# Token sums of a hybrid attention layer: the subtractions beside values and context on VectorE, and the first pair's sums from reloaded f32 rows

## The chip, the cores and the metric

The kernel runs on one core of one Trainium2 chip. The metric is the device time of one execution in microseconds, as the median of several runs. TensorE (PE) multiplies; VectorE (DVE), ScalarE (ACT) and GpSimd (POOL) do the elementwise work; the queues of SyncE (SP) and ACT issue the DMAs.

## What is computed

One layer of a diffusion backbone over 2048 latent tokens and 256 context tokens, all in f32, with model width 1024:

```python
h_lat = _rmsnorm(x, norm_g[i]) * (1.0 + scale) + shift
h_ctx = _rmsnorm(ctx, norm_g[i]) * (1.0 + scale_c) + shift_c
na_q, na_k, na_v, na_g, r_q, r_k, r_v, r_g = _split_proj(h_lat @ w_in)
cna_q, cna_k, cna_v, cna_g, cr_q, cr_k, cr_v, cr_g = _split_proj(h_ctx @ w_in)
...
y_lat = jnp.concatenate([y_na, y_ret], axis=-1) @ w_out
x = x + gate * y_lat
```

Between projection and output stand a neighbourhood attention over a 2-D window plus the context keys, and a two-directional retention. The change lies wholly in the projection `h @ w_in`, whose columns are eight groups of 512.

## The kernel before

**Three products for one.** TensorE multiplies f32r operands. So that little is lost, each f32 operand is split into a high part, a cast to f32r, and a low part, the operand minus the cast; a product is hi·hi + hi·lo + lo·hi. The cast is made by ACT, the subtraction by DVE or POOL. For a weight tile of 256 columns this is `w_split`: two casts and two subtractions of 128x1024 (L348, L350), one for each half of the 1024 rows. Its argument `lo` says by bits which half's subtraction goes to POOL: `lo=1` puts the first on POOL and the second on DVE, `lo=0` both on DVE.

**Blocks of tokens.** The latent tokens are four blocks of 512. `window(b)` normalises and projects the keys of block b (window 4: the context's keys). The normalised f32 rows of each block are also stored to HBM as `hS[b]`. Blocks 0 and 1 stay in the pool `hx` as hi and lo, blocks 2 and 3 pass through the pool `hy`, which has two buffers of each name (`hhi`, `hlo`), and are reloaded later from `hS`.

**The order after the windows.** It is written out by hand, all in program order on each engine:

1. *Context units* (`CTXU`): four projections of the context tokens, then its values with two weights. A unit is one call of a generator that issues matmuls and yields; here each has 8 yields of 6 matmuls (128x256). Before each unit the next weight is split (L350) and another one is loaded by SP into the raw tiles `st` (L176).
2. *Values of blocks 0 and 1*: 8 units (`u_v`). A unit's result is cast by ACT (L415), its low part made by DVE (L416), and 8 DMAs on SP store it (`vB`, L425). These tiles `o` have two buffers.
3. *First Strassen pass*, blocks 0 and 1: six sets of 256 columns. A set needs 7 products of 12 matmuls (128x512) where 8 would stand. It multiplies sums of weight quarters (`w_sums`, L667, L668, L677 to L685) with sums of token quarters, the four tiles `T`.
4. *Values of blocks 3 and 2*: 8 units, two for block 3 with each of two weights, then block 2.
5. *Second Strassen pass*, blocks 2 and 3, six sets. Then attention starts, with further projections between its steps.

**The token sums.** With A and B the pair's blocks and the index for the half of the rows, they are d = B2 − B1 (third tile), d + A1 (second), A2 − (d + A1) (fourth) and B1 − A1 (first), each split again into a cast and a subtraction. They are cut into pieces, and `pump` puts one piece into the program every few yields of the units.

- *First pair*, `h_sums(T, 0, 1)`: blocks 0 and 1 are there as hi and lo, so each sum adds the differences of the hi and of the lo parts: DVE takes hi (L620, L630, L639, L651), POOL the lo difference (L621, L650), DVE adds them (L622, L631, L640, L652), ACT casts (L611), and DVE or POOL subtracts (L612). Ten pieces start at the context's values, one every 6 yields.
- *Second pair*, `h_sums_raw(T2, 2, 3)`: the reloads bring the f32 rows into the tiles that will hold lo, so sums are taken from them directly (L545, L560, L564, L569, L591) before `re_split` casts a block (L520) and overwrites it with its low part (L521), half on DVE and half on POOL. The opening piece (differences and the split of block 3) stands in the last set of the first pass; ten more are spread over the value units, one every 4 yields.

**Other work on the same engines.** In the passes and in the second value units DVE, ACT and POOL also scale the output weights by the gate (`wo_mul`, L792 to L797; its loads L777 are on SP).

## Time and profile before

| | us |
|---|---|
| median of 3 runs (1387.51 to 1389.98) | 1388.68 |
| the profiled execution's own time | 1390.82 |
| its span, first to last instruction | 1388.9 |
| TensorE busy in the span | 1320.5 |
| DVE busy | 841.9 |
| POOL busy | 655.0 |
| ACT busy | 606.8 |

The mean granted clock of TensorE is 0.99. In time order: window 4 ends near 162, context units to 197, values to 243, the first pass to 375, values to 430, the second pass to 558 us. Idle time with the name that ended it is in the views of waits and timelines. A group's row gives line, engine, operation, out<-in, shape, count, busy us and mean ns. An engine name with a q is its queue, which issues DMAs or waits.

### The profile page before, as it was taken

The numbers are of one execution on the slowest core, as the hardware profiler recorded it, in microseconds if no ns is written. First come the engines' busy times: TensorE is split into PE (matmuls) and PEld (weight loads), VectorE is DVE, ScalarE is ACT, GpSimd is POOL, SyncE is SP. The second block draws the span as 40 slices with busy tenths as digits, with TensorE's granted clock in tenths as the row PEclk, the third lists the DMA queues.
The fourth block names the chain that finished last, engine by engine and source line by source line (L and its number), as shares of the span: only waits on it lengthen the run. The fifth ranks groups of instructions, "written<-read, shape, count | busy, mean of one in ns | idle before, by whom it ended". The sixth has DMA issues, their size and how long they took to land.

```text
span 1388.9 us, 23101 instructions
## 1 busy us (share of the span) xinstructions
PE 1320.5 (95%) x8236; PEld 1152.0 (83%) x8236; DVE 841.9 (61%) x1422; ACT 606.8 (44%) x1261; POOL 655.0 (47%) x603
## 2 busy tenths in 40 slices
PE   6989999899988999999999999999999899999997
PEld 2477999678787678998899889789999789888886
DVE  5786365677584864377767777777654634344445
ACT  4454332233343334365556464656652234423332
POOL 4452435455455566345535373665433145454342
PEclk9999999999999999999999999999999999999999
DMA  9587655656567666886676897667628888555533
GB/s 310 176 279 242 208 178 126 176 180 212 182 175 208 217 220 209 260 216 183 176 216 194 211 236 215 183 179 206 174 84 262 252 286 281 181 168 168 159 114 129
DMA packets 233302, 278.86 MB, mean 201 GB/s; under 512 B 17122, under 2 KB 180066, under 8 KB 232163
## 3 DMA queue, kind: packets, MB, share of 16 engines
q1 hardware_dynamic: 201858, 221.01, 54.7%
q10 hardware_dynamic: 31328, 56.37, 11.4%
q8 instruction: 66, 1.08, 0.3%
q14 instruction: 50, 0.40, 0.1%
HBM read 188.19 MB, written 89.13 MB: 200 GB/s over the span
## 4 chain that ended last, share of the span: by engine, by line
PE 63%; DVE 12%; DMA 8%; issue 6%; POOL 4%; ACT 4%; SPq 3%; ACTq 0%; DVEq 0%; POOLq 0%
PE mm L377 13%; PE mm L1487 11%; PE mm L714 11%; PE mm L366 7%; PE sS L1047 4%; PE tr L1074 3%; PE po L1095 3%; DMA vB<-o 2%; PE mm L1210 2%; PE mm L314 2%; PE tr L1076 2%; PE po L1097 1%; SPq L425 1%; DMA v<-rvS 1%; PE mm L1399 1%
## 5 line engine op out<-in xcount | busy, mean ns | idle before, releaser
L377 PE MATMUL mm<-whi,hhi 128*128 128x256 f32 x768 | 224.7, 293 | 0.0
L377 PE MATMUL mm<-whi,hlo 128*128 128x256 f32 x768 | 217.7, 284 | 4.9 <-DVE hlo L521 4.3
L377 PE MATMUL mm<-wlo,hhi 128*128 128x256 f32 x768 | 217.5, 283 | 1.8 <-DVE wlo L350 1.1
L1078 ACT CAST pt<-tr 128x640 fp32r<-128x640 f32 (+1 forms) x128 | 95.6, 747 | 162.8 <-PE tr L1076 157.0
L1084 DVE TENSOR_TENSOR pt<-tr,pt 128x640 fp32r<-128x640 f32 (+1 forms) x128 | 113.9, 890 | 80.6 <-ACT pt L1078 79.5
L1067 POOL TENSOR_SCALAR sp<-sp,stt 128x640 f32<-128x640 f32 (+2 forms) x128 | 103.2, 809 | 107.9 <-DVE stt L1066 78.4
L377 PEld LDWEIGHTS mm<-whi,hlo 128*128 128x128 f32 x768 | 147.2, 192 | 5.9 <-DVE hlo L521 5.1
L377 PEld LDWEIGHTS mm<-wlo,hhi 128*128 128x128 f32 x768 | 146.7, 191 | 2.2 <-DVE wlo L350 1.3
L377 PEld LDWEIGHTS mm<-whi,hhi 128*128 128x128 f32 x768 | 146.8, 191 | 0.1
L1056 DVE CUSTOM_DVE_ANT_0 sp<-sS,nb 128x640 f32<-128x640 f32 (+2 forms) x128 | 105.5, 824 | 32.3 <-DMA q<-qS 19.1
L1061 ACT ACTIVATE sp<-sp,stt 128x640 f32<-128x640 f32 (+2 forms) x128 | 107.4, 839 | 20.6 <-DVE stt L1056 19.4
L350 POOL TENSOR_TENSOR wlo<-st,whi 128x256 fp32r<-128x256 f32 (+1 forms) x79 | 85.1, 1090 | 62.4 <-ACT whi L348 51.2
L366 PE MATMUL mm<-hhi,whi 128*128 128x512 f32 x256 | 107.2, 419 | 0.0
L366 PE MATMUL mm<-hlo,whi 128*128 128x512 f32 x256 | 101.1, 395 | 6.0 <-DVE hlo L283 2.3
L714 PE MATMUL mm<-hhi,whi 128*128 128x512 f32 x336 | 100.2, 401 | 4.7 <-POOL whi L668 2.0
L1047 PE MATMUL sS<-k,q 128*128 128x256 f32 (+3 forms) x512 | 99.1, 315 | 5.8 <-DVE stt L1056 5.6
L366 PE MATMUL mm<-hhi,wlo 128*128 128x512 f32 x256 | 101.2, 395 | 0.3 <-DVE wlo L350 0.3
L1496 DVE TENSOR_TENSOR xt<-mm,xt 128x512 f32<-128x512 f32 x64 | 43.8, 686 | 87.1 <-PE mm L1487 87.1
L1487 PE MATMUL mm<-wor,y 128*128 128x512 f32 x384 | 95.6, 398 | 1.1 <-DVE xt L1496 1.1
L1047 PEld LDWEIGHTS sS<-k,q 128*128 128x128 f32 x512 | 82.8, 188 | 12.9 <-DVE stt L1056 9.1
L1487 PE MATMUL mm<-won,y 128*128 128x512 f32 x336 | 89.9, 406 | 0.0
L668 POOL TENSOR_TENSOR wlo<-st,wlo 128x512 fp32r<-128x512 f32 x36 | 52.0, 1444 | 69.3 <-ACT wlo L667 69.3
(274 smaller groups left out, 3159.2 us busy)
## 6 DMA issues: line engine op xcount, KB each, us to landing
st<-in_w_in_dram SPq DMA_DIRECT2D x64, 512.0 KB
q<-qS SPq DMA_DIRECT2D x64, 256.0 KB
k<-kS SPq DMA_DIRECT2D x16, 576.0 KB
kS<-o SPq DMA_DIRECT2D x16, 512.0 KB
vB<-o SPq DMA_DIRECT2D x64, 128.0 KB
qS<-o ACTq DMA_DIRECT2D x16, 512.0 KB
hlo<-hS SPq DMA_DIRECT2D x16, 512.0 KB
woS<-g ACTq DMA_DIRECT2D x32, 256.0 KB
```

The source lines that it names most:

```text
L350: eng.tensor_tensor(l, r, f(h), ALU.subtract)
L366: nc.tensor.matmul(pm[:, :n], ww[:, k, cs], h[:, k, :], start=(k == 0 and i == 0), stop=(k == KC - 1 and i == 2))
L377: nc.tensor.matmul(pm[:, t * WG:(t + 1) * WG], h[:, k, o:o + P], ww[:, k, :], start=(k == 0 and i == 0), stop=(k == KC - 1 and i == 2))
L668: nc.gpsimd.tensor_tensor(t[:, 1], r, f(t)[:, 0], ALU.subtract)
L714: nc.tensor.matmul(pm, ww[:, k, :], hh[:, k, :], start=(k == 0 and i == 0), stop=(k == KH - 1 and i == 2))
L1047: nc.tensor.matmul(o, hd["q"][i][:, hl, j * P:(j + 1) * P], k, start=(hl == 0), stop=(hl == 1))
L1056: nc.vector.tensor_tensor_reduce(T["sp"][:, :n], T["s"], nbz[big][:, o:o + n], -1.0, 3e38, ALU.add, ALU.min, T["st"][:, 0:1])
L1061: nc.scalar.activation(sp[:, :n], sp[:, :n], AF.Exp, bias=st[:, 0:1], scale=-1.0, accum_out=st[:, 1:2])
L1067: nc.gpsimd.tensor_scalar(sp[:, :n], sp[:, :n], st[:, 2:3], 0.0, ALU.mult, ALU.add)
L1078: nc.scalar.copy(pt[:, :ng_ + 2, 0, :], tr[:, :ng_ + 2, :])
L1084: nc.vector.tensor_tensor(pt[:, :n, 1, :], tr[:, :n, :], f(pt)[:, :n, 0, :], ALU.subtract)
L1487: nc.tensor.matmul(pm, yy[:, k, :], ww[:, k, sl], start=(k == 0 and i == 0), stop=(k == 3 and i == 2))
```

## The change

Four edits:

1. The weight splits beside values and context have `lo=0`: both subtractions on DVE. Those are the four of the context units, the second value weight, and the plain weights ahead of and in the second values (`plain_next`).
2. `raw_rows` reloads the f32 rows of blocks 1 and 0 from `hS` at the start of window 4, eight DMAs of 0.5 MB on SP, into two `hy` tiles. The first pair's sums are taken from those rows.
3. One function `h_sums` makes both pairs' sums. Every addition and subtraction of it is on DVE, POOL has none. The first pair has 11 pieces, which start at the fourth context unit, one every 5 yields.
4. `re_split` is cut into `re_cast` (ACT) and `re_sub`, with pieces of their own for the second pair: block 3's four casts, the two differences and its four subtractions still open in the last set of the first pass; block 2's casts stand in the piece `rest` and its subtractions in two pieces `subs` behind it. There are 13 pieces after the opening one, every 4 yields.

```diff
+            if b == 4 and n == 0:
+                frows.extend(raw_rows())
...
+    def raw_rows():
+        res = []
+        for b, name in ((1, "hhi"), (0, "hlo")):
+            t = hy.tile([P, KC, 512], F32, name=name)
+            for k in (0, 4, 2, 6):
+                nc.sync.dma_start(t[:, k:k + 2, :], hS[b][:, k:k + 2, :])
+            res.append(t)
+        return res
...
-    def re_split(b, ks, eng):
+    def re_cast(b, ks):
         hi, lo = blk[b]
         nc.scalar.copy(hi[:, ks, :], f(lo)[:, ks, :])
+
+    def re_sub(b, ks, eng=nc.vector):
+        hi, lo = blk[b]
         eng.tensor_tensor(lo[:, ks, :], f(lo)[:, ks, :], f(hi)[:, ks, :], ALU.subtract)
...
+    def h_sums(T, A, B, rows=None):
+        xb, xa = rows or (f(blk[B][1]), f(blk[A][1]))
+        hb = xb if rows else f(blk[B][0])
+        V = nc.vector.tensor_tensor
...
+        def low(key, src):
+            for c in range(2):
+                V(t[key][:, 1, pairs(c), :], src(c), f(t[key])[:, 0, pairs(c), :], ALU.subtract)
+
+        def diff():
             tile_(0, "hhi", F32)
+            if not rows:
+                for n in (0, 2, 1, 3):
+                    re_cast(B, pairs(n))
             for c in range(2):
+                V(d(c), xb[:, pairs(c + 2), :], xb[:, pairs(c), :], ALU.subtract)
+            if not rows:
+                for n in range(4):
+                    re_sub(B, pairs(n))
...
+        def rest():
             for c in range(2):
+                V(e[c], e[c], xb[:, pairs(c), :], ALU.add)
+            for n in range(4):
+                re_cast(A, pairs(n))
+
+        def subs(m):
+            for n in (2 * m, 2 * m + 1):
+                re_sub(A, pairs(n))
...
+        res = [diff, third, lambda: low(3, d), second, fourth, first]
+        if not rows:
+            res += [rest, lambda: subs(0), lambda: subs(1)]
+        return res + [open2, open4, lambda: low(4, d4), open1, lambda: low(1, ec)]
...
-            res.append(w_split(wcur.pop(0), lo=1))
+            res.append(w_split(wcur.pop(0), lo=0))
...
-    for c0, u in CTXU:
-        wn = w_split(wcur.pop(0), lo=1)
+    for n, (c0, u) in enumerate(CTXU):
+        if n == 3:
+            pump.update(y=0, every=5, q=h_sums(T, 0, 1, frows))
+        wn = w_split(wcur.pop(0), lo=0)
...
-    pump.update(y=0, every=6, q=h_sums(T, 0, 1))
...
-    hooks[21].append(lambda: raws[0]())
+    hooks[21].append(lambda: raws.pop(0)())
...
-    pump.update(y=3, every=4, q=raws[1])
+    pump.update(y=2, every=4, q=raws)
```

What the program's order becomes at three places. First SP's queue around window 4, as one piece of the difference; `kS` are stores of keys (those of 256x1x512 of window 3, of 256x1x256 of window 4), `st` raw weights, `hS` the stored rows:

```order
 L176 DMA st<-in_w_in_dram 128x4x256 x2
 L150 DMA kS_64<-o 256x1x512
+L518 DMA hhi<-hS_88 128x1024 x4
+L518 DMA hlo<-hS_87 128x1024 x4
 L150 DMA kS_61<-o 256x1x256
 L150 DMA kS_62<-o 256x1x256
```

The eight reloads stand ahead of all stores of window 4, and these ahead of the next twelve loads of weights.

Second DVE from the context units on, before; L416 is the low part of a value unit, L771 opens the gate's sum:

```order
L350 TENSOR_TENSOR wlo<-st,whi 128x1024 x5
L620 TENSOR_TENSOR hhi<-hhi 128x1024
L622 TENSOR_TENSOR hhi<-hhi 128x1024
L612 TENSOR_TENSOR hlo<-hhi,hlo 128x1024
L416 TENSOR_TENSOR o<-mm,o 128x4x128
L620 TENSOR_TENSOR hhi<-hhi 128x1024
L622 TENSOR_TENSOR hhi<-hhi 128x1024
L612 TENSOR_TENSOR hlo<-hhi,hlo 128x1024
L416 TENSOR_TENSOR o<-mm,o 128x4x128
L771 MEMSET gacc 128x1024
```

and now:

```order
L350 TENSOR_TENSOR wlo<-st,whi 128x1024 x8
L568 TENSOR_TENSOR hhi<-hhi 128x1024 x2
L350 TENSOR_TENSOR wlo<-st,whi 128x1024 x2
L560 TENSOR_TENSOR hlo<-hhi,hlo 128x1024 x2
L416 TENSOR_TENSOR o<-mm,o 128x4x128
L579 TENSOR_TENSOR hhi<-hhi,hlo 128x1024 x2
L416 TENSOR_TENSOR o<-mm,o 128x4x128
L733 MEMSET gacc 128x1024
```

The sums begin ahead of the last weight split, both halves of every split are here, and by the time of L733 (the old L771) the second sum (L579, the old L630 and L631) is done as well.

Third DVE over the value units of block 3, up to the low parts of block 2. Before, behind that set's additions (L538 low parts of sums, L560, L564, L569 the sums, L521 low parts of a reloaded block, L350 a weight split):

```order
L538 TENSOR_TENSOR hlo<-hhi,hlo 128x1024
L560 TENSOR_TENSOR hhi<-hhi,hlo 128x1024 x2
L416 TENSOR_TENSOR o<-mm,o 128x4x128
L350 TENSOR_TENSOR wlo<-st,whi 128x1024
L564 TENSOR_TENSOR hhi<-hlo,hhi 128x1024 x2
L569 TENSOR_TENSOR o_3178<-hhi,hlo 128x1024
L569 TENSOR_TENSOR e<-hhi,hlo 128x1024
L416 TENSOR_TENSOR o<-mm,o 128x4x128
L792 TENSOR_TENSOR wraw<-wraw,gacc 128x512
L521 TENSOR_TENSOR hlo<-hlo,hhi 128x1024 x2
```

and now, behind the third sum's low part (L560, x2 in place of the one L538; L579, L583, L588, L592 are the sums, L536 low parts of a reloaded block, L754 is the old L792):

```order
L416 TENSOR_TENSOR o<-mm,o 128x4x128
L350 TENSOR_TENSOR wlo<-st,whi 128x1024 x2
L579 TENSOR_TENSOR hhi<-hhi,hlo 128x1024 x2
L583 TENSOR_TENSOR hhi<-hlo,hhi 128x1024 x2
L416 TENSOR_TENSOR o<-mm,o 128x4x128
L754 TENSOR_TENSOR wraw<-wraw,gacc 128x512
L588 TENSOR_TENSOR o_3212<-hhi,hlo 128x1024
L588 TENSOR_TENSOR e<-hhi,hlo 128x1024
L592 TENSOR_TENSOR o_3212<-o_3212,hlo 128x1024
L592 TENSOR_TENSOR e<-e,hlo 128x1024
L416 TENSOR_TENSOR o<-mm,o 128x4x128
L536 TENSOR_TENSOR hlo<-hlo,hhi 128x1024 x4
```

All four low parts of block 2 are here (two were on POOL before), and one more eviction (L416), the second half of the weight split and the two additions L592 stand ahead of them.

More of the change, by code (lines that the diff above doesn't have):

```diff
@@ L532, in tile_, with cast @@
             t[key] = hy.tile([P, 2, KH, 512], dt, name=name)
-        def cast(key, c, d):
-            nc.scalar.copy(t[key][:, 0, pairs(c), :], d)
-        def low(key, c, d, eng):
-            eng.tensor_tensor(t[key][:, 1, pairs(c), :], d, f(t[key])[:, 0, pairs(c), :], ALU.subtract)
         d = lambda c: t[0][:, 0, pairs(c), :]
-        def open_b():
+        d4 = lambda c: t[0][:, 1, pairs(c), :]
+        ec = lambda c: e[c]
+        def cast(key, src):
+            for c in range(2):
+                nc.scalar.copy(t[key][:, 0, pairs(c), :], src(c))
@@ L543, in open_b @@
+        def low(key, src):
+            for c in range(2):
+                V(t[key][:, 1, pairs(c), :], src(c), f(t[key])[:, 0, pairs(c), :], ALU.subtract)
+        def diff():
             tile_(0, "hhi", F32)
+            if not rows:
+                for n in (0, 2, 1, 3):
+                    re_cast(B, pairs(n))
             for c in range(2):
-                V.tensor_tensor(d(c), lb[:, pairs(c + 2), :], lb[:, pairs(c), :], ALU.subtract)
-            for n in (0, 2, 1, 3):
-                re_split(B, pairs(n), (V, G)[n // 2])
@@ L549, in h_sums_raw, with third, second @@
-        d4 = lambda c: t[0][:, 1, pairs(c), :]
-        def p1():
+                V(d(c), xb[:, pairs(c + 2), :], xb[:, pairs(c), :], ALU.subtract)
+            if not rows:
+                for n in range(4):
+                    re_sub(B, pairs(n))
+        def third():
             tile_(3, "hlo")
+            cast(3, d)
+        def second():
             for c in range(2):
-                cast(3, c, d(c))
-            low(3, 0, d(0), V)
-            low(3, 1, d(1), G)
-        def p2():
+                V(d(c), d(c), xa[:, pairs(c), :], ALU.add)
@@ L559, in p2, with fourth, first @@
+        def fourth():
             for c in range(2):
-                V.tensor_tensor(d(c), d(c), xa[:, pairs(c), :], ALU.add)
-        def p3():
-            for c in range(2):
-                V.tensor_tensor(d4(c), xa[:, pairs(c + 2), :], d(c), ALU.subtract)
-        def p4():
+                V(d4(c), xa[:, pairs(c + 2), :], d(c), ALU.subtract)
+        def first():
             e[0], e[1] = env["st"].tile([P, 2, 512], F32, name="o3", bufs=1), wo["p"].tile([P, 2, 512], F32, name="e")
             for c in range(2):
-                V.tensor_tensor(e[c], hb[:, pairs(c), :], xa[:, pairs(c), :], ALU.subtract)
@@ L571, in p5 @@
-        def p5(m):
-            for n in (m, m + 2):
-                re_split(A, pairs(n), (V, G)[n // 2])
-        def both(key, src, first):
-            for c in range(2):
-                cast(key, c, src(c))
-            for c in range(2):
-                low(key, c, src(c), (V, G)[c ^ first])
-        def p7():
-            tile_(4, "hlo")
-            both(4, d4, 1)
-        def p8():
-            tile_(2, "hhi")
-            both(2, d, 0)
-        def p9():
-            for c in range(2):
-                V.tensor_tensor(e[c], e[c], lb[:, pairs(c), :], ALU.add)
@@ L593, in p10, with open2, open4 @@
-        def p10():
+                V(e[c], hb[:, pairs(c), :], xa[:, pairs(c), :], ALU.subtract)
+        def rest():
+            for c in range(2):
+                V(e[c], e[c], xb[:, pairs(c), :], ALU.add)
[4 more added lines that the diff above has]
+                re_sub(A, pairs(n))
+        def open2():
+            tile_(2, "hhi")
+            cast(2, d)
+        def open4():
+            tile_(4, "hlo")
+            cast(4, d4)
+            low(2, d)
```

64 lines of the change are left out of this document (7 added, 57 removed).

## The prediction, as it was recorded before the run

> **What bounds the kernel now.** First the page's busy time by engine and its chain of waits, to see which engine the work queues behind.
>
> ```profile
> PE 1320.5 (95%) x8236; PEld 1152.0 (83%) x8236; DVE 841.9 (61%) x1422; ACT 606.8 (44%) x1261; POOL 655.0 (47%) x603
> PE 63%; DVE 12%; DMA 8%; issue 6%; POOL 4%; ACT 4%; SPq 3%; ACTq 0%; DVEq 0%; POOLq 0%
> ```
>
> TensorE is busy for 95% of the span, and its instructions are the same before and after. So the change can be worth only what TensorE loses in the stages it touches. The table of stretches shows where that is, by the number of matmuls (the x behind PE's time) against the length.
>
> ```profile
> core 0: us, PE busy (x) PEld busy (x) DVE busy (x) ACT busy (x) POOL busy (x), PEclk, DMA share, GB/s
> 152.50:165.00 12.50, 12.50 (x107) 12.50 (x106) 1.82 (x6) 5.28 (x8) 5.66 (x3) 1.00 0.39 134
> 220.00:243.00 23.00, 23.00 (x194) 23.00 (x193) 10.86 (x11) 5.97 (x11) 14.76 (x10) 1.00 0.51 122
> 243.00:290.00 47.00, 39.69 (x150) 29.93 (x148) 28.04 (x32) 14.62 (x27) 24.16 (x18) 0.89 0.59 179
> 290.00:355.00 65.00, 65.00 (x280) 52.29 (x278) 46.76 (x56) 22.42 (x40) 29.74 (x23) 1.00 0.53 178
> 361.00:373.00 12.00, 12.00 (x54) 9.69 (x53) 5.64 (x5) 6.73 (x7) 5.19 (x2) 1.00 0.95 348
> 375.00:430.00 55.00, 48.43 (x382) 47.42 (x383) 44.33 (x32) 21.31 (x28) 28.37 (x12) 0.97 0.61 174
> 430.00:492.00 62.00, 54.49 (x223) 41.89 (x223) 39.18 (x46) 22.68 (x41) 33.64 (x26) 0.97 0.67 220
> ```
>
> Undisturbed, the value units (128x256 matmuls) run at 23.00/194 = 0.1186 us each, and the Strassen sets (128x512) at 65.00/280 = 0.2321. At these rates three stretches are too long. **A**, the start of the first Strassen pass, held 150 matmuls, 34.8 us of work in 47: 12.2 lost. **B**, the second value units: 382, 45.3 of 55: 9.7 lost. **C**, the start of the second pass: 223, 51.8 of 62: 10.2 lost. Together 32.1 us, idle time and the matmuls at a lower granted clock behind it (0.89 in A). The waits of TensorE from 190 to 500 us name the late producers.
>
> ```profile
> PE mm L714 <- ACT wlo L667: 7.1, 3, 3.3
> PE mm L377 <- DVE hlo L521: 4.3, 3, 2.3
> PE mm L714 <- POOL wlo L668: 3.0, 4, 1.1
> ```
>
> They are parts of the weight sums (L667, L668) in A and C and the low parts of a reloaded block (L521) in B: all work that stands behind the token sums on ACT, DVE and POOL. Why these run late is seen where DVE and POOL meet, in the timelines of the two:
>
> ```profile
> 182.21 2.39 POOL L350 TENSOR_TENSOR wlo<-st,whi 128x1024 fp32r<-128x1024 f32 x1 [3.94 <-ACT whi L348]
> 183.16 2.52 DVE L350 TENSOR_TENSOR wlo<-st,whi 128x1024 fp32r<-128x1024 f32 x1 [3.81 <-ACT whi L348]
> 366.56 1.23 DVE L350 TENSOR_TENSOR wlo<-st,whi 128x1024 fp32r<-128x1024 f32 x1 [4.95 <-PE mm L714]
> 366.59 3.45 POOL L350 TENSOR_TENSOR wlo<-st,whi 128x1024 fp32r<-128x1024 f32 x1 [5.97 <-PE mm L714]
> ```
>
> The same subtraction took DVE 2.52 us when POOL had begun first: POOL ended at 184.60, DVE 1.08 later. It took 1.23 when DVE began first, and then POOL needed 3.45. They exclude each other for whole instructions. A subtraction moved from POOL to DVE therefore replaces about 2.3 us of that turn-taking with 1.2.
>
> **The change part by part.** *First pair's sums.* The row of the last old piece's wait, and where A's weight part then stood on ACT:
>
> ```profile
> L652 DVE TENSOR_TENSOR o<-o,e 128x512 f32<-128x512 f32 x4 | 2.8, 692 | 7.7 <-POOL e L650 7.6
> 250.09 0.62 ACT L611 CAST hhi<-o 128x512 fp32r<-128x512 f32 x1 [6.35 <-DVE o L652]
> 251.09 0.62 ACT L667 CAST wlo<-st 128x512 fp32r<-128x512 f32 x1
> 258.43 0.58 ACT L415 CAST o<-mm 128x512 fp32r<-128x512 f32 x1 [6.24 <-DMA vB<-o]
> ```
>
> TensorE left the value units at 243.1, the first start of a Strassen product:
>
> ```profile
> L714 PE MATMUL mm<-hhi,whi x336: 387/392/792, 243.1 to 552.0; 128*128 128x512 f32 x168
> ```
>
> ACT cast the last unit's result only at 258.43, 15 us behind, and the part L667 stood behind the sums' cast at 250.09. After the change DVE holds 16 subtractions and additions of 128x1024 for this pair, 16 x 1.23 = 19.7 us, and POOL none. They start one value-width unit earlier (at the fourth context unit) and are due over 55 yields; a yield is six matmuls, 0.71 us, so five yields, 3.6 us, hold one piece of 2.5 us on DVE: it keeps up. The last piece then comes before the fourth value unit's end, near 220, instead of 250. The part that was waited for follows the sixth of the eight value units; these end at 243.1, so it ends at 243.1 − 2 x 5.69 = 231.7, and TensorE asks for the part two products (24 x 0.2321 = 5.6) into the pass, near 248.7: even at 3 us for cast and subtraction it is covered. The eviction at 258.43 comes near 244, with its stores earlier by as much. I leave 1.0 us of A's 12.2 for contention among the weight sums, which still subtract on POOL: −11.2. If the cover fails (stores from vB late by themselves) half of it stays.
>
> *Second pair: the first block.* Rows of DVE there, and TensorE's first value matmul:
>
> ```profile
> L521 DVE TENSOR_TENSOR hlo<-hlo,hhi x4: 1481/3153/3414, 372.2 to 404.1; 128x1024 fp32r<-128x1024 f32 x4
> L564 DVE TENSOR_TENSOR hhi<-hlo,hhi x2: 1209/1210/1210, 394.7 to 395.9; 128x1024 f32<-128x1024 f32 x2
> L545 DVE TENSOR_TENSOR hhi<-hlo x2: 1210/1567/1924, 369.2 to 371.0; 128x1024 f32<-128x1024 f32 x2
> 374.63 0.28 PE L377 MATMUL mm<-whi,hhi 128*128 128x256 f32 x1
> 378.82 0.68 DVE L750 TENSOR_TENSOR o<-mm,e 128x512 f32<-128x512 f32 x1
> 382.33 0.68 DVE L760 TENSOR_TENSOR o<-mm,e 128x512 f32<-128x512 f32 x1
> 385.16 1.23 DVE L538 TENSOR_TENSOR hlo<-hhi,hlo 128x1024 fp32r<-128x1024 f32 x1 [2.15 <-ACT hlo L535]
> ```
>
> The two differences start at 369.2 as before (a buffer comes free then). With POOL silent they end at 371.6 and the four subtractions at 372.8, 374.0, 375.3 and 376.5. TensorE arrives at 374.6 and takes one every 0.71 us: nothing is lost there, and the six additions that began at 378.82 begin at 376.5, ending near 380.6.
>
> *Second pair: the second block.* Its subtractions now stand behind more DVE work. From 380.6: 2.0 us until the first cast comes (2.15 before), then 12 operations (two each of the third sum's low part, the weight split, second, fourth, first and rest) at 1.21, three evictions at 0.69, one 0.7 for the output weights, and the first subtraction, 1.21: 2.0 + 14.5 + 2.1 + 0.7 + 1.2 = 20.5, so 401.1. TensorE asks at 374.6 + 4 units x 48 x 0.1186 = 397.4: 3.7 us of waiting, then three further ones at 1.21 against 0.71, 1.5 more. The weight split in the same queue ends its first half near 386.9, asked for at 386.0: 0.8. B is left with 6.0 of 9.7: −3.7. Queued behind these waits is nothing but TensorE.
>
> *Start of the second pass.* Rows of ACT and DVE:
>
> ```profile
> 386.42 6.65 DVE L560 TENSOR_TENSOR hhi<-hhi,hlo 128x1024 f32<-128x1024 f32 x2
> 393.00 0.68 DVE L416 TENSOR_TENSOR o<-mm,o 128x512 fp32r<-128x512 f32 x1
> 437.93 0.58 ACT L415 CAST o<-mm 128x512 fp32r<-128x512 f32 x1 [4.11 <-DMA vB<-o]
> 438.41 0.62 ACT L667 CAST wlo<-st 128x512 fp32r<-128x512 f32 x1
> 452.46 0.69 DVE L792 TENSOR_TENSOR wraw<-wraw,gacc 128x512 f32<-128x512 f32 x1 [7.97 <-DMA wraw<-in_w_out_dram]
> ```
>
> Both waits are stores of value units that came late, and one load queued behind them on SP. The first value unit's eviction stood behind L538 and 6.65 us of L560; it moves from 393.0 to 380.6 + 2.0 + 2.4 + 0.7 = 385.7, so the stores run some 7 us earlier. ACT's last eviction, 8 us behind the 430 at which TensorE left these units, comes about 3 us behind the 374.6 + 45.5 + 6.0 = 426.1 at which it will: an estimate, from the stores' earlier start. I leave 2.5 of C's 10.2: −7.7.
>
> *The reload at window 4.* Eight DMAs of 0.5 MB enter SP's queue between the last store of keys of window 3 and those of window 4:
>
> ```profile
> 152.65 11.42 SPq L150 DMA_DIRECT2D kS<-o  x5
> 360.63 4.80 SPq L854 DMA_DIRECT2D hlo<-hS  x8
> hlo<-hS SPq DMA_DIRECT2D x16, 512.0 KB
> 159.85 0.37 ACT L386 CAST o<-mm 128x256 fp32r<-128x256 f32 x1 [0.58 <-PE mm L366]
> 162.97 2.00 ACT L348 CAST whi<-st 128x1024 fp32r<-128x1024 f32 x2
> 165.00 2.57 DVE L350 TENSOR_TENSOR wlo<-st,whi 128x1024 fp32r<-128x1024 f32 x1 [1.47 <-ACT whi L348]
> ```
>
> Eight reloads of the same size, issued at 360.63, ran at 348 GB/s (the stretch from 361 to 373). At that rate 4.2 MB take 12.1 us, and with the 0.5 MB ahead of them they land near 167.5. If the stores of window 4 come behind them, the tile that the eviction of 159.85 writes (two buffers) comes free only near 168; the cast of 162.97 follows at 169.2, and the first half of the weight split is ready at 169.2 + 1.0 + 1.2 = 171.4, where TensorE wants it at 168.2: +3.2. If stores and reloads share the engines, nothing is lost (0.39 of them were busy); if the next weight loads, behind those stores on SP, come late too, about 5 more. I take 3.2, the case that needs no second delay. The Trainium skill ("DMA: Bandwidth & Descriptors", section "Queues, rings and completion order") says that each DMA engine consumes a ring's descriptors in order; no row above shows it, and by it the term would be the 3.2, without it 0 and the whole forecast lower by as much.
>
> *Casts and subtractions in separate parts* for the later reloads keep the engine and the order: 0.
>
> Sum: −11.2 − 3.7 − 7.7 + 3.2 = −19.4 us. The profiled execution took 1390.8, so it would take 1371.4; it lies 2.1 above the median of 1388.7, which becomes 1369.3. All that follows the second pass moves with it, since TensorE stays at 66 us of work in each such stretch.
>
> **The rivals.**
>
> *Weight sums stay late* (0.20). ACT's 6.24 and 4.11 us waits for stores speak for it: if the stores set the pace by themselves, half of A and of C remains, 5.1 and 2.6 more than I left: 1369.3 + 7.7 = 1377.
>
> *No queue at window 4 and a quicker second block* (0.12). Without the 3.2, and with the second block's wait halved, 1369.3 − 3.2 − 2.6 = 1363.5.
>
> *DVE saturated* (0.08). DVE is busy 44.3 of 55 us in B, and nine operations move onto it there. If its time were its own work, 9 x 1.23 = 11 us would be added to TensorE's wait in B, and the same late evictions would return 4 to C: 1369.3 + 15 = 1384. Against it: the 44.3 contains the turns of POOL (3.15 in the median of L521 against 1.21). The Trainium skill ("Perfetto Trace Analysis", section "Optimizing Scalar/DVE Operations") would offload to GpSimd where DVE is saturated, and adds that between these two it might not help.
>
> *Slower: the weight loads fall behind* (0.06). Each context unit splits 1 MB of weights per 5.7 us, 184 GB/s, on top of stores; after the 4.2 MB the queue may not catch up. It decides if each of the six weights split here lands 4 us late again, as then 24 us are lost: 1393. Against it: 348 GB/s were seen, so over 100 GB/s remain to recover.
>
> **How the numbers follow.** My forecast has 0.54, the rivals 0.46. The range 1360 to 1381 holds the forecast (no queue at window 4 to 8 us there: 1366 to 1375), the first two rivals and what lies around them; the last two lie outside. A measurement of this kernel tells about 0.2%, 2.8 us. Faster by more than that: 0.54 + 0.20 + 0.12 and half of the third rival, 0.90; within it 0.04; slower 0.06.
>
> **What would show it.** Right: A's stretch (243 to 290, moved with the stage) holds some 195 matmuls; no POOL subtraction stands between the context and the first pass but L668's; DVE's 128x1024 operations all take about 1.2 us; the wait on the second block's low parts is 3 to 5 us; TensorE waits once near 168 us for a weight part. Wrong: if the DVE operations stay at 2.5 with POOL idle, if weight parts are still waited for in A, or if TensorE waits at every context unit.

## The result, and the profile after

The changed kernel took 1373.88 us (median of 4 runs, 1372.97 to 1375.66) where the kernel before took 1388.10 beside it: a ratio of 0.990, 95% interval 0.988 to 0.992, 14.2 us less. The forecast of 1369.3 was 4.6 us too low; the time lies in its range and on the side that it gave 0.90. The profiled execution took 1372.97 (span 1371.2) against 1390.82. All times here and below are of fast runs; one of the six runs of the kernel "subtractions ahead" took 3223.66 us in the slow state and is left out.

The page of the kernel after, busy time by engine and chain of waits:

```profile
PE 1315.6 (96%) x8236; PEld 1151.6 (84%) x8236; DVE 822.9 (60%) x1432; ACT 607.4 (44%) x1259; POOL 585.4 (43%) x573
PE 61%; DMA 12%; DVE 9%; POOL 6%; issue 6%; ACT 4%; SPq 2%; ACTq 0%; POOLq 0%; DVEq 0%
```

DVE has ten instructions more and is busy for 19 us less; POOL has 30 fewer and 70 us less. Two things are mixed in this: DVE waits for fewer turns of POOL (an addition of the second pair took 3.37 us on average before, L560, and takes 1.22 now, L579), and the first pair needs fewer operations (counted in 128x1024 pieces, 18 on DVE and 10 on POOL before, 16 on DVE now). In the chain DVE falls from 12% to 9%, and DMA takes its place, 12% for 8%.

Where did the time go? TensorE's work in a stage is fixed, so the time from its first matmul in one stage to its first in the next can be set side by side. The starts are read from TensorE's timelines (before 151.11, 243.12, 374.63, 430.17 and, behind the four stages, 557.86; after 149.88, 247.85, 366.23, 417.28 and 541.82); the undisturbed time is the stage's matmuls at the prediction's 0.1186 us (128x256) and 0.2321 us (128x512).

| stage (matmuls) | undisturbed | before | after | difference | forecast |
|---|---|---|---|---|---|
| window 4, context, first values (768) | 91.1 | 92.0 | 98.0 | +6.0 | +3.2 |
| first pass (504) | 117.0 | 131.5 | 118.4 | −13.1 | −11.2 |
| second values (384) | 45.5 | 55.5 | 51.1 | −4.5 | −3.7 |
| second pass (504) | 117.0 | 127.7 | 124.5 | −3.2 | −7.7 |

The four stages save 14.8 us (406.75 to 391.94; differences are taken before rounding); of the 17.7 us between the two spans, 1.2 lie ahead of them and 1.7 behind, where the change does nothing. The stretches of the kernel after that answer to those of before (context, start of the first pass, second values, second pass):

```profile
165.00:176.00 11.00, 7.05 (x45) 6.63 (x44) 3.21 (x4) 4.20 (x6) 0.00 (x0) 0.84 0.73 235
247.00:294.00 47.00, 47.00 (x209) 38.45 (x208) 30.59 (x37) 15.89 (x28) 20.98 (x15) 1.00 0.56 189
366.20:417.40 51.20, 48.52 (x386) 47.83 (x385) 40.34 (x40) 22.76 (x30) 11.48 (x5) 0.97 0.73 206
417.30:542.00 124.70, 119.41 (x508) 94.16 (x507) 77.94 (x94) 47.76 (x83) 70.36 (x52) 1.00 0.63 209
```

The start of the first pass holds 209 matmuls in the 47 us that held 150, at a granted clock of 1.00 for 0.89. The first row is new: 45 matmuls, 5.3 us of work, in 11.0. TensorE's waits from 150 to 560 us (us in total, times, longest) name what is late now:

```profile
PE mm L377 <- ACT whi L348: 3.2, 1, 3.2
PE mm L377 <- DVE hlo L536: 2.7, 2, 2.5
PE mm L676 <- POOL wlo L630: 1.9, 3, 0.6
PE mm L676 <- DVE o L712: 1.6, 1, 1.6
PE mm L676 <- ACT wlo L629: 1.4, 3, 0.9
PE mm L377 <- DVE wlo L350: 0.8, 1, 0.8
```

Three places are left. **At the context**, the reload. SP's queue, then ACT around it:

```profile
152.03 2.46 SPq L518 DMA_DIRECT2D hhi<-hS  x4
154.53 2.12 SPq L518 DMA_DIRECT2D hlo<-hS  x4
156.90 13.48 SPq L150 DMA_DIRECT2D kS<-o  x4
155.77 0.37 ACT L386 CAST o<-mm 128x256 fp32r<-128x256 f32 x1 [2.47 <-PE mm L366]
168.32 0.37 ACT L386 CAST o<-mm 128x256 fp32r<-128x256 f32 x1 [10.29 <-DMA kS<-o]
169.28 2.00 ACT L348 CAST whi<-st 128x1024 fp32r<-128x1024 f32 x2
```

The first store of window 4 was issued at 156.90, behind the eight reloads; the eviction that needs its buffer waited 10.29 us and started at 168.32. **In the second values**, DVE's order ahead of the low parts of block 2:

```profile
387.12 1.22 DVE L592 TENSOR_TENSOR o<-o,hlo 128x1024 f32<-128x1024 f32 x1
388.26 1.22 DVE L592 TENSOR_TENSOR e<-e,hlo 128x1024 f32<-128x1024 f32 x1
390.39 0.69 DVE L416 TENSOR_TENSOR o<-mm,o 128x512 fp32r<-128x512 f32 x1 [0.92 <-DMA vB<-o]
391.00 4.62 DVE L536 TENSOR_TENSOR hlo<-hlo,hhi 128x1024 fp32r<-128x1024 f32 x4
```

TensorE wants the first of them at 389.7 and starts at 392.27, 2.5 us later. **At the start of the second pass**, ACT, DVE and SP:

```profile
421.98 0.59 ACT L415 CAST o<-mm 128x512 fp32r<-128x512 f32 x1 [4.65 <-DMA vB<-o]
422.46 0.62 ACT L629 CAST wlo<-st 128x512 fp32r<-128x512 f32 x1
435.22 0.69 DVE L754 TENSOR_TENSOR wraw<-wraw,gacc 128x512 f32<-128x512 f32 x1 [6.73 <-DMA wraw<-in_w_out_dram]
401.77 28.43 SPq L425 DMA_DIRECT2D vB<-o  x32
430.30 0.36 SPq L739 DMA_DIRECT2D wraw<-in_w_out_dram  x1
```

The same two waits as before, and of like length: ACT's last eviction of the values waits 4.65 us for stores (4.11 before), and DVE 6.73 (7.97) for the next rows of the output weights, whose load is issued only at 430.30, behind 32 stores.

### The profile page after: what moved, and what is told of

It is laid out like the page before. It is cut to its first block, busy times and chain, and to the rows that moved or that the text cites. A ratio compares the mean times of both kernels' runs of the same rounds, so it can differ in the third digit from the quotient of the medians.

```text
span 1371.2 us, 23069 instructions
## 1 busy us (share of the span) xinstructions
PE 1315.6 (96%) x8236; PEld 1151.6 (84%) x8236; DVE 822.9 (60%) x1432; ACT 607.4 (44%) x1259; POOL 585.4 (43%) x573
## 4 chain that ended last, share of the span: by engine, by line
PE 61%; DMA 12%; DVE 9%; POOL 6%; issue 6%; ACT 4%; SPq 2%; ACTq 0%; POOLq 0%; DVEq 0%
PE mm L377 15%; PE mm L1450 11%; PE mm L676 8%; PE mm L366 6%; PE sS L1010 4%; PE tr L1037 3%; PE po L1058 3%; PE mm L1173 2%; DMA v<-rvS 2%; PE tr L1039 2%; PE po L1060 1%; DMA woS<-g 1%; POOL g L757 1%; PE mm L314 1%; PE mm L1362 1%
## 5 line engine op out<-in xcount | busy, mean ns | idle before, releaser
L1024 ACT ACTIVATE sp<-sp,stt 128x640 f32<-128x640 f32 (+2 forms) x128 | 107.4, 839 | 20.1 <-DVE stt L1019 19.1
L630 POOL TENSOR_TENSOR whi<-st,whi 128x512 fp32r<-128x512 f32 x48 | 62.9, 1332 | 107.3 <-ACT whi L629 106.2
L676 PE MATMUL mm<-hhi,whi 128*128 128x512 f32 x336 | 98.2, 395 | 2.0 <-DVE o L712 1.6
L630 POOL TENSOR_TENSOR wlo<-st,wlo 128x512 fp32r<-128x512 f32 x36 | 51.2, 1423 | 81.2 <-ACT wlo L629 81.2
```

The source lines that it names most:

```text
L630: nc.gpsimd.tensor_tensor(t[:, 1], r, f(t)[:, 0], ALU.subtract)
L676: nc.tensor.matmul(pm, ww[:, k, :], hh[:, k, :], start=(k == 0 and i == 0), stop=(k == KH - 1 and i == 2))
L1024: nc.scalar.activation(sp[:, :n], sp[:, :n], AF.Exp, bias=st[:, 0:1], scale=-1.0, accum_out=st[:, 1:2])
```

## The experiments

Each kernel starts from the changed one, with one edit unless the text says more. The stages are those of the table above, from one profiled execution each; "sum" is over the four, and the last column the rest of that span behind them. The kernel before ran beside each one on the same chip (1388.1 to 1390.1 us), so compare ratios rather than medians. The two rows of the changed kernel differ by up to 0.7 us in a stage and by 2.5 behind the stages, which says how much one execution can tell.

| kernel | median | ratio to before [95%] | context etc. | first pass | second values | second pass | sum | rest |
|---|---|---|---|---|---|---|---|---|
| before | 1388.1 | 1 | 92.0 | 131.5 | 55.5 | 127.7 | 406.8 | 831.1 |
| after | 1373.9 | 0.9901 [0.9880, 0.9922] | 98.0 | 118.4 | 51.1 | 124.5 | 391.9 | 829.4 |
| after, again | 1376.2 | 0.9899 [0.9879, 0.9919] | 98.7 | 118.4 | 51.5 | 124.1 | 392.7 | 831.9 |
| first pair alone | 1384.2 | 0.9957 [0.9943, 0.9971] | 97.4 | 118.4 | 55.5 | 128.4 | 399.7 | 829.7 |
| second pair alone | 1383.1 | 0.9954 [0.9937, 0.9971] | 92.0 | 132.6 | 50.7 | 123.7 | 398.9 | 833.5 |
| reloads spread | 1369.5 | 0.9851 [0.9829, 0.9874] | 94.5 | 118.4 | 50.7 | 123.2 | 386.8 | 830.2 |
| reloads from ACT's queue | 1374.2 | 0.9884 [0.9861, 0.9907] | 97.7 | 118.4 | 51.7 | 122.4 | 390.2 | 829.1 |
| half back on POOL | 1379.8 | 0.9927 [0.9908, 0.9946] | 99.3 | 118.4 | 58.9 | 118.5 | 395.1 | 832.4 |
| output weights later | 1381.4 | 0.9945 [0.9927, 0.9962] | 98.5 | 118.4 | 50.5 | 124.0 | 391.4 | 836.1 |
| additions behind | 1374.8 | 0.9890 [0.9865, 0.9914] | 98.2 | 118.4 | 51.6 | 122.8 | 390.9 | 830.8 |
| output weights from ACT's queue | 1372.7 | 0.9876 [0.9854, 0.9899] | 98.6 | 118.4 | 51.4 | 121.0 | 389.4 | 832.4 |
| subtractions ahead | 1372.9 | 0.9885 [0.9863, 0.9908] | 98.0 | 118.4 | 46.4 | 126.1 | 388.9 | 829.2 |
| three edits | 1368.4 | 0.9847 [0.9827, 0.9868] | 95.9 | 118.4 | 46.4 | 126.0 | 386.7 | 829.6 |
| four edits | 1366.8 | 0.9848 [0.9824, 0.9872] | 93.5 | 118.4 | 46.4 | 124.7 | 383.0 | 829.4 |

The theory at the start: the change removes DVE's turns with POOL, each of its parts works in its own stage, and what is lost anew at the context is the stores' wait behind the reload. The rivals: the second pair gains only through the first, the queue's order is not what costs, and the loss of the second pass is only handed on.

**The two halves of the change.** In the first, `h_sums_raw` of before serves the second pair; in the second, the old `h_sums` serves the first pair and nothing is reloaded. Each keeps the weight splits of its own half.

```diff
-        raws.extend(h_sums(T2, 2, 3))
+        raws.extend(h_sums_raw(T2, 2, 3))
```

> Only the first pair's part of the change: its sums from reloaded rows in the context, all subtractions of the values' and the context's weights on DVE up to the first values unit; the second pair is summed as before. Theory (the parts are independent): the 13 us that TensorE lost at 243 to 290 us go, the reload costs 6 us, and the 9.5 and 10.9 us lost by the second pair stay: near 1381 us with the kernel before at 1389, ratio near 0.9945. Rival (loss only moves on, since DVE and GpSimd together have too much to do before the attention): the second pair's loss grows by several us and the time is 1384 or more, ratio over 0.997.

```diff
-            if b == 4 and n == 0:
-                frows.extend(raw_rows())
...
+    pump.update(y=0, every=6, q=h_sums_old(T, 0, 1))
```

> Only the second pair's part of the change (its casts and subtractions in separate parts, all on DVE, and the second values unit's weight split on DVE); the first pair is summed as before, without the reload. Theory (the parts are independent): the loss at 243 to 290 us stays at 13 us, there is no 6 us at the context, and the second pair's two losses fall from 20.4 to about 12.8 us: near 1381.5 us with the kernel before at 1389, ratio near 0.9945. Rival (the second pair gains only because the first pair's work is over sooner): 1386 or more, ratio over 0.998.

The stages answer as the theory said: without the second half the two later stages stay at 55.5 and 128.4, without the first half the first two stay at 92.0 and 132.6. The profiles' sums fall by 7.0 and 7.8 us, together the 14.8 of the whole change. In time the halves came out at 1384.2 and 1383.1 us, above the theory's 1381 and 1381.5; the first reaches the time that its rival named, 1384 or more, but its ratio, 0.9957, lies nearer the theory's 0.9945 than the rival's 0.997. The ratios, 6.0 us (0.0043 of 1389.5) and 6.4, add to 12.4, within the interval of the whole (10.8 to 16.7). By the stages the parts are independent, and the reload's price is 5 to 6 us: 98.0 and 97.4 with it, 92.0 without.

**The reload, spread.** One of the eight loads at every fourth step of window 3.

```diff
-            if b == 4 and n == 0:
-                frows.extend(raw_rows())
+            if b == 3 and n % 4 == 0:
+                raw_row(n // 4)
```

> The same eight reloads, one every four matmul groups of window 3 instead of all together at the start of window 4. Theory (the stores of window 4 stand behind the burst of reloads in SP's ring): the eviction that waited 10.3 us for its store's tile no longer waits, TensorE's loss of about 5.9 us near 170 us goes, nothing else changes: about 1368 us, 5 to 6 below the changed kernel. Rival (the 4.2 MB cost the same wherever they are moved, since the DMA engines are shared): the loss moves into window 3, and the time stays within 1.5 us of 1374.

3.4 of the 6 us go, and the ratio is 0.985. The eviction on ACT in window 4, from the timeline:

```profile
159.73 0.37 ACT L386 CAST o<-mm 128x256 fp32r<-128x256 f32 x1 [5.90 <-DMA kS<-o]
```

TensorE's waits from 150 to 180 us:

```profile
PE mm L377 <- POOL wlo L350: 2.0, 2, 1.4
```

The eviction still waits for a store, 5.90 us where the theory had none and the changed kernel 10.29, and the 4.0 us of TensorE's waits there are 2.0. The loss did not move into window 3, as the rival had it: from TensorE's L209 matmuls in that window to window 4's first matmul it is 27.0 us in both kernels (123.44 to 150.41 here, 122.91 to 149.88 after). But the DMA engines were still full when window 4 began, at 1.06 of the stretch from 153 to 158 us, which fits the 2.5 us that are left.

**The reload from ACT's queue**, at the old place.

```diff
-                nc.sync.dma_start(t[:, k:k + 2, :], hS[b][:, k:k + 2, :])
+                nc.scalar.dma_start(t[:, k:k + 2, :], hS[b][:, k:k + 2, :])
```

> The same eight reloads at the same place, issued on ACT's queue instead of SP's. Theory (order in the ring): stores of keys and weight loads on SP are no longer behind them, they share the engines packet by packet; the 10.3 us wait of the eviction falls under 4 us, TensorE loses at most 1.5 us near 170: 1368 to 1370 us. Rival (bandwidth, not order): stores of window 4 come as late as before, since the engines are full until 167 us; 1373 to 1375 us.

The theory missed, and the time is the rival's, 1374.2: the context takes 97.7 for 98.0, ratio 0.988. ACT and its queue, and SP's queue, in that kernel:

```profile
153.98 1.80 ACTq L518 DMA_DIRECT2D hhi<-hS  x4
155.82 4.36 ACTq L518 DMA_DIRECT2D hlo<-hS  x4
160.28 0.37 ACT L386 CAST o<-mm 128x256 fp32r<-128x256 f32 x1 [5.72 <-DMA hhi<-hS]
165.71 0.37 ACT L386 CAST o<-mm 128x256 fp32r<-128x256 f32 x1 [5.06 <-DMA kS<-o]
155.31 17.97 SPq L150 DMA_DIRECT2D kS<-o  x5
```

The stretch of 15 us in which the reload runs:

```profile
153.00:168.00 15.00, 12.82 (x102) 12.23 (x101) 1.54 (x3) 3.22 (x5) 0.89 (x1) 1.00 1.01 371
```

Two things took the queue's place. ACT itself issues until 160.18 (the first wait, put down to `hS`, ends there). And the store issued on SP at 155.31, with no reload ahead of it in its queue, let the eviction of 165.71 go only 10.4 us later; behind the reloads it was 11.4 (156.90 to 168.32). The last row fits this: the DMA engines were busy for 1.01 of the stretch. So a place in another queue frees little while 4.2 MB fill the engines. How much of the 11.4 us the order costs by itself stays open, since ACT's 6.2 us of issuing are mixed in, and the store of 155.31 is twice as large (it is window 3's last).

The view of the DMA queues from 153 to 166 us gives packets, MB and share of the engines; q10 is ACT's queue, q1 SP's:

```profile
q10 hardware_dynamic: 878, 3.23, 67.2%
q1 hardware_dynamic: 1250, 1.49, 33.2%
```

The Trainium skill ("DMA: Bandwidth & Descriptors", section "Queues, rings and completion order") says that an engine takes turns between the queues that have work for it. The shares agree that both were served at once, SP's queue with a third. What of the 10.4 us is this share, and what the rest of the 1.49 MB in SP's queue, is not separated.

**Half of the low parts back on POOL**, in both pairs and in the weight splits, which tests whether the engine matters or only the new order of the pieces.

```diff
-                V(t[key][:, 1, pairs(c), :], src(c), f(t[key])[:, 0, pairs(c), :], ALU.subtract)
+                (nc.vector, nc.gpsimd)[c].tensor_tensor(t[key][:, 1, pairs(c), :], src(c), f(t[key])[:, 0, pairs(c), :], ALU.subtract)
...
-        wn = w_split(wcur.pop(0), lo=0)
+        wn = w_split(wcur.pop(0), lo=1)
```

> The changed kernel with only the engine undone: the second half of every low part (sums, block splits, weight splits beside values and context) goes back to POOL; pieces, their order and the reloaded rows stay. Theory (DVE and POOL exclude each other, so a subtraction on POOL holds both for 2.3 us where DVE needs 1.2): DVE operations of 2.4 to 3.4 us return, the second value units lose 4 to 6 us more, the start of the first pass at most 2: 1378 to 1382 us. Rival (the gain comes from fewer and earlier operations, the engine does not matter): within 1.5 us of 1374.

The time is the expected one, 1379.8, but the interval of its ratio, from 0.9908, overlaps that of the changed kernel, up to 0.9922; the stages are 2.4 to 3.2 us longer than in the two profiles of the latter. A row of DVE and one of POOL, from the timeline:

```profile
396.59 3.39 DVE L592 TENSOR_TENSOR e<-e,hlo 128x1024 f32<-128x1024 f32 x1
395.66 6.52 POOL L536 TENSOR_TENSOR hlo<-hlo,hhi 128x1024 fp32r<-128x1024 f32 x2 [1.22 <-ACT hhi L532]
```

TensorE's longest wait from 150 to 560 us:

```profile
PE mm L377 <- DVE hlo L536: 8.2, 3, 5.2
```

The addition that takes 1.22 us with POOL silent takes 3.39 beside its subtractions, and the second values grow from 51.1 to 58.9 us. But the second pass then loses hardly anything, 118.5: the loss of the second pair came earlier. Its two stages together took 177.4 us here and 175.6 after.

And the first pass does not change, 118.4 in both, where up to 2 us more were expected. The first pair's sums end at 227.2 us here, 23.5 ahead of the pass. After, they end at 223.2, 24.7 ahead; before, they ended at 252.1, 8.9 us into it. So with half of its low parts on POOL the first pair is still early enough: its 13.1 us need the sums to be done in time, and this run does not show that they need POOL to be free.

**The output weights later.** Their twelve parts of the second pass move from every second step to steps 7 to 23.

```diff
-    for n in range(12):
-        hooks[2 * n].append(halves.pop(0))
+    for n in (7, 8, 10, 11, 13, 14, 16, 17, 19, 20, 22, 23):
+        hooks[n].append(halves.pop(0))
```

> The changed kernel with the twelve steps that scale the output weights in the second pass put later: none in its first seven steps, the two sets whose results are scaled and split. The work is the same. Theory (what is left at the start of the second pass, about 7.8 us, comes from these steps: DVE stands 6.7 us on a load of output weights that SP issues late, and later their subtraction on POOL delays the weight parts): 1.5 to 2.5 us remain, 1368 to 1369 us. Rival (late stores of value units are the cause, as the prediction had it): at least 6 us remain there, 1372 to 1374 us.

This missed on the other side: 1381.4, slower than after. TensorE's longest wait:

```profile
PE mm L377 <- ACT o L452: 5.9, 1, 5.9
```

ACT at that time:

```profile
556.68 0.62 ACT L756 CAST g<-wraw 128x512 fp32r<-128x512 f32 x1 [8.35 <-DMA ggS<-o]
559.10 0.58 ACT L452 COPY o<-mm 128x512 f32<-128x512 f32 x1
```

The second pass as a whole is as long as after, 124.0: the waits of its first sets fell, as the theory had it (one of 0.62 us at 425, the next not before 484), and others stood in its later ones. The last part then waited 8.35 us on ACT, ahead of the first evictions of the next stage (L452), which costs the rest of the span 6.7 us (836.1 for 829.4).

**The additions behind the subtractions**, in the second pair's first values.

```diff
-        def rest():
-            for c in range(2):
-                V(e[c], e[c], xb[:, pairs(c), :], ALU.add)
+        def casts():
             for n in range(4):
                 re_cast(A, pairs(n))
...
-            res += [rest, lambda: subs(0), lambda: subs(1)]
+            res += [casts, lambda: subs(0), lambda: subs(1), rest]
```

> One edit to the changed kernel: in the second pair, the two additions that finish the fourth sum run behind the two groups of low-part subtractions of its first block, not ahead of them; the casts stay ahead. Theory: TensorE's 4.8 us of wait at 392 us for a low part of that block is the two 1.2 us additions and the eight subtractions queued on DVE, so about 2.4 us of it goes: near 1371.5 us with the kernel before at 1389, ratio near 0.988. Rival: the wait is set by when the casts on ACT come, or the later additions make the fourth sum late in the second pass and the loss only moves there: 1373.5 to 1375, ratio 0.990 to 0.991.

The rival was right, 1374.8 us: the stage takes 51.6 for 51.1. DVE's rows:

```profile
392.34 0.69 DVE L416 TENSOR_TENSOR o<-mm,o 128x512 fp32r<-128x512 f32 x1 [3.62 <-ACT o L415]
392.95 4.62 DVE L536 TENSOR_TENSOR hlo<-hlo,hhi 128x1024 fp32r<-128x1024 f32 x4
```

With the additions gone DVE only waits longer, 3.62 us for 0.92, for ACT's half (L415) of the eviction of a values piece, whose second half stands ahead of the four subtractions in DVE's order. ACT's half itself starts at 391.73, behind the four casts (387.01 to 390.90) and a wait of 0.82 us for stores. So the eviction holds them, which the next run tests.

**The subtractions ahead of that eviction**: `subs(0)` and `subs(1)` in the same step as the casts, and the two additions behind them again.

```diff
+        def casts():
+            for n in range(4):
+                re_cast(A, pairs(n))
+            for m in range(2):
+                subs(m)
...
-            res += [rest, lambda: subs(0), lambda: subs(1)]
+            res += [casts, rest]
```

> One edit to the changed kernel: in the second pair, all eight low-part subtractions of the first block (as four instructions) stand in the same step as its casts, the two additions behind them. On DVE the four then stand ahead of the eviction of a values piece (line 416) that they stood behind, and that waited for its buffer until 390.4 us. Theory: that eviction, not the additions, held the low parts back, so TensorE's 4.8 us at 392 us falls to about 1 us: near 1370 us with the kernel before at 1389, ratio near 0.9873. Rival (the eviction, now behind the four, comes later and TensorE waits for its accumulator, or the same time is lost at the start of the second pass, whose sums follow): 1373 to 1375 us, ratio 0.990 to 0.991.

> The changed kernel once more, as the standard for the two runs beside it: 1373 to 1375 us with the kernel before at 1389, ratio 0.988 to 0.992.

The changed kernel itself gave the ratio expected of it, 0.9899 (its time of 1376.2 us lies 1.2 above the range, with the kernel before at 1390.1).

The place answers in full: the second values take 46.4 us, 0.9 over the undisturbed time, and that wait of TensorE is gone. (It was 2.7 us; the 4.8 of the expectation are nearer the whole loss of the stage, 5.6.) DVE, and ACT at the start of the second pass:

```profile
388.10 4.62 DVE L536 TENSOR_TENSOR hlo<-hlo,hhi 128x1024 fp32r<-128x1024 f32 x4
392.65 0.68 DVE L416 TENSOR_TENSOR o<-mm,o 128x512 fp32r<-128x512 f32 x1
421.88 0.59 ACT L415 CAST o<-mm 128x512 fp32r<-128x512 f32 x1 [4.57 <-DMA vB<-o]
```

TensorE's longest wait from 300 to 560 us:

```profile
PE mm L680 <- ACT wlo L633: 3.8, 1, 3.8
```

But 1.6 of the 4.7 us come back in the second pass (124.5 to 126.1). Measured from the start of the second values, TensorE arrives there 4.6 us sooner (46.4 for 51.1) and ACT's last eviction of the values only 1.1 (54.7 for 55.8): it waits for the stores, and the weight part for it. In time the edit is inconclusive, ratio 0.9885 [0.9863, 0.9908] beside 0.9899 [0.9879, 0.9919] for the changed kernel.

**The output weights' rows from ACT's queue**, one step later.

```diff
-            wo_load(a["w_out"][(k + 1) * P:(k + 2) * P, :])
+            defer(1, lambda: wo_load(a["w_out"][(k + 1) * P:(k + 2) * P, :], nc.scalar))
```

> One edit to the changed kernel: the next rows of the output weights are loaded from ACT's queue, one step later and behind their own two stores, in place of SP's, where the load of 430.3 us stood behind 32 stores of values. Theory: DVE then no longer waits 6.7 us for those rows at 435.2 us, its weight sums come about 2.6 us sooner, and TensorE's waits at 442.8, 446.6 and 448.0 us (1.8, 1.1 and 0.9 us) fall to about 1 us in all: near 1371 us with the kernel before at 1389, ratio near 0.988. Rival (the waits of this pass are handed on from one group of four steps to the next, as with the output weights moved): the loss comes back at 450 to 480 us and the time stays at 1373.5 to 1375, ratio 0.990 to 0.991.

DVE's step for these rows:

```profile
432.28 1.77 DVE L754 TENSOR_TENSOR wraw<-wraw,gacc 128x512 f32<-128x512 f32 x1 [3.99 <-POOL whi L630]
```

TensorE's waits in the second pass:

```profile
PE mm L676 <- ACT wlo L629: 1.3, 1, 1.3
PE mm L676 <- POOL wlo L630: 0.6, 1, 0.6
```

The step starts 2.9 us sooner (4.6 from the start of the pass), the wait for L712 is gone, and the second pass is 3.5 us shorter in the profile. The ratio, 0.9876 [0.9854, 0.9899], points the same way, but its interval overlaps that of the changed kernel.

**Three and four edits together.** Three: reloads spread, subtractions ahead, output weights' rows from ACT's queue. Four: also half of the values' stores from ACT's queue.

```diff
-                defer(1 + r, lambda dst=dst[r], src=o[64 * r + k0:64 * r + k0 + cw]: nc.sync.dma_start(dst, src))
+                defer(1 + r, lambda dst=dst[r], src=o[64 * r + k0:64 * r + k0 + cw], q=(nc.sync, nc.scalar)[r]: q.dma_start(dst, src))
```

> Three edits to the changed kernel together: the eight reloads spread over the third context window, the four subtractions ahead of the eviction, and the output weights' rows loaded from ACT's queue. If their savings add (4.5, 3.5 and 1 to 3 us): near 1364 us with the kernel before at 1389, ratio near 0.982. Rival (the second and third edit only hand the loss on within the second pass): no better than the spread alone, 1369 us, ratio 0.985.

> The three edits together, and a fourth: of the eight stores of each values piece (line 425), the four of the second half go out from ACT's queue in place of SP's. With the subtractions ahead of the eviction, the loss at 392 us came back as 6.9 us at 422 to 427 us, where ACT's last eviction of the values waited 4.6 us for a buffer that those stores still read. Theory: SP's issuing of eight stores of 0.4 us each, one behind the other, paces those buffers, so half of them on another queue frees the buffer about 2 us sooner, and over the last pieces the 6.9 us fall to about 2: near 1363.5 us with the kernel before at 1389, ratio near 0.9815. Rival (the stores' transfers take the time, not their issue, or their issue on ACT delays its casts by as much): 1368 to 1372 us, ratio 0.985 to 0.988.

Both expectations of added savings failed. Three edits give 0.985, the ratio of the spread alone; their gain in the second values is again answered by a second pass of 126.0 us. Four give the same ratio; the profile is 3.7 us shorter over the four stages, which the runs do not confirm. ACT with four edits:

```profile
415.23 0.59 ACT L415 CAST o<-mm 128x512 fp32r<-128x512 f32 x1 [0.47 <-DMA vB<-o]
417.22 0.62 ACT L631 CAST wlo<-st 128x512 fp32r<-128x512 f32 x1 [1.40 <-DVE st L649]
424.06 0.62 ACT L631 CAST wlo<-st 128x512 fp32r<-128x512 f32 x1 [4.14 <-DMA woS<-g]
```

The last eviction does come sooner, 5 us behind TensorE's end of the values at 410.1 in place of 8.3 (421.88 against 413.6). The weight casts behind it then wait for a weight sum on DVE, and later for ACT's own issues and stores. Every version that beats the kernel after by more than its interval spreads the reloads; the edits to the second pair add nothing that can be measured.

## Why the prediction was right, and where its sizes were off

**The mechanism: seen in the rows, not isolated in the first pair.** DVE's operations that stood beside POOL's take 1.22 us where they took up to 3.4, and 3.39 again with half of the low parts back on POOL. The rival "DVE saturated" falls: with all of it on DVE the second values got shorter, and DVE is busy for 822.9 us with 20 instructions more, for 825.5 with half back. But the half put back costs 2.4 to 3.2 us in the four stages, 1.8 of them in the second pair's two, and nothing in the first pass. The largest gain, 13.1 us, comes from the first pair's sums being done ahead of the pass. How much of that is POOL's silence, how much the 16 operations in place of 28, and how much the earlier and denser pieces, no run separates: that part of the mechanism is argued.

**First pass.** The forecast was −11.2, with 1.0 left; nothing was left, −13.1. The last piece ends at 223.2 (forecast "near 220"). Half of the rival "weight sums stay late" falls here: ACT's last eviction comes 0.2 us behind TensorE's end of the values (248.05 against 247.85) where it came 15 behind, so its wait in that place was the sums' lateness passed on, not the stores' own pace.

**Second values.** −4.5 for −3.7, in part by luck. The working named the right wait and its time: the first subtraction ends 26.0 us behind the start of the stage (392.2), forecast 26.5. But of the 5.6 us lost only 2.7 are waits, where the working counted 6.0; the rest are matmuls at a granted clock of 0.70 in the 5.7 us behind the wait (392.3 to 398), a loss that the working has no term for. It saw that one eviction more (L416) stands ahead of the subtractions, but priced it at its own 0.69 us. It needs ACT's half first, which stands behind the four casts on ACT, so DVE could not pass it before 391.0. Moving the two additions that the working counted at 2.4 us gained nothing while it stood there; moving the subtractions ahead of both gained the stage 4.7.

**Second pass: the step that failed.** The working left 2.5 of C's 10.2, a saving of 7.7 for stores that start some 7 us earlier; −3.2 came. The stores did start earlier: the first value unit's 10.7 us behind the start of the second values (376.95) where it was 19.1 (393.70), and ACT's last eviction 55.8 behind it where it was 63.3, against 54.5 in the working. TensorE arrives 4.5 us sooner itself, so the eviction is 4.7 behind it (421.98 against 417.3, forecast 3) where it was 7.8. TensorE's longest waits in the first and the second group of products, before and after:

```profile
439.08 0.50 PE L714 MATMUL mm<-hhi,wlo 128*128 128x512 f32 x1 [3.28 <-ACT wlo L667]
460.01 0.47 PE L714 MATMUL mm<-hhi,whi 128*128 128x512 f32 x1 [1.73 <-DVE o L750]
424.49 0.50 PE L676 MATMUL mm<-hhi,wlo 128*128 128x512 f32 x1 [0.62 <-POOL wlo L630]
442.76 0.47 PE L676 MATMUL mm<-hhi,whi 128*128 128x512 f32 x1 [1.56 <-DVE o L712]
```

All waits of the first group fell from 3.9 to 0.8 us, about the 3.2 that came. Those behind it stayed: 3.5 us before (443 to 492), 4.5 after (428 to 479). The working had both as one, "stores of value units that came late, and one load queued behind them on SP". The load is what followed too little. It is issued 13.0 us into the pass (430.30) where it was 16.9 (447.08), again behind the values' stores, and DVE waits 6.73 us for it, 7.97 before. That DVE's step, not the evictions, keeps the second group late is borne out by two runs: with its load on ACT's queue the wait for L712 is gone and the pass is 3.5 us shorter in the profile, and with the steps put later nothing over 0.62 us is waited for until 484. In neither did the whole kernel get faster by more than its interval.

The rival "weight sums stay late" would have left 5.1 of the second pass's loss, where 7.5 stayed, but it had them as weight sums behind the stores' own pace, and those are in time here. The pace of the stores does show when TensorE comes sooner still: with the subtractions ahead its wait at that place is 3.8 us. What paces that start once the stores are relieved too is not settled. A weight sum and ACT's issues come up next in the trace, and no run took those away alone.

**Reload.** The sign and the step were right: the eviction gets its buffer at 168.3 (forecast "near 168"), the casts start at 169.28 (169.2). The stage began 1.2 us earlier than before, though, so all this is some 1.4 us later than the working had it, and the two waits for the first half of the split, 3.2 us for the cast and 0.8 for its low part, make 4.0 where the term was 3.2. Another 1.7 us are matmuls at a lower granted clock behind them (0.84 over the stretch, 11.0 − 5.3 = 5.7 us lost), for which the working has no term. That it is the queue's order, as assumed, is not shown: from ACT's queue the reload cost as much. So the wait came near the term for a reason that the runs do not confirm.

The sum was −19.4, the four stages gave −14.8: the second pass (4.5) and the reload (2.8) came out worse, the first pass (1.9) and the second values (0.8) better. Of the marks named ahead, the start of the first pass holds 209 matmuls (195 forecast), POOL has only L630 (the old L668) between the context and the first pass, and DVE's 128x1024 operations there take 1.2 us. TensorE's wait at the context is there, from 167.2 to 170.4. The wait on the second block's low parts is 2.7 us, under the 3 to 5 named.

## What to carry to other kernels

Cost a moved instruction by what stands ahead of it in its engine's order, and ask of each such neighbour what it waits for: an eviction of 0.7 us that needed another engine's half first held four subtractions, and taking away the 2.4 us of additions ahead of it gained nothing while it stood there. A burst of loads is paid by the stores beside it: here it cost the context as much from either queue, and 2.5 us in place of 6 when it was spread over the window ahead. And when several waits follow one another, price each by its own cause: the stores came earlier and the first wait of the second pass went with them, but the load behind them was still late, and its wait stayed. Where a stage has a pace of its own, as the stores of the last values have, a saving ahead of it is passed on once TensorE comes sooner than they do.

## What the runs showed that was not expected

A DMA queue of ACT costs ACT its own time: eight loads of 0.5 MB held its sequencer for 6.2 us (153.98 to 160.18) while the engines were full, 4.4 of them for the last four, where SP issued all eight in 4.6 (152.03 to 156.65). And a wait of TensorE can cost more than its length: 4.0 us of waits at the context came with 1.7 us more at a lower granted clock, and behind 2.5 us of waiting in the second values the granted clock was 0.78 (392.3 to 395) and 0.63 (395 to 398) before it was 1.00 again.
